# The first layer's modulation made feature tile by feature tile, with the first projection unit summed over open banks as its tiles come

## The chip, the cores and the metric

The kernel runs on one core of one Trainium2 chip (trn2). The metric is the device time of one execution in microseconds (us). The core's engines run side by side, each through its own list of instructions in a fixed order: TensorE (PE in the profile, PEld for its weight loads), VectorE (DVE), ScalarE (ACT), GpSimd (POOL) and SyncE (SP), which issues the transfers. An instruction that waits for another engine holds up all that stands behind it on its own engine.

## What is computed

The reference is one step of a two-layer trunk over 640 tokens of 1024 features: 512 sample tokens and 128 context tokens. In each layer the tokens are normalised, scaled and shifted by a modulation, and multiplied by a wide projection `w_in`; three mixers follow, then an output projection, a second modulated norm and a feed-forward part. The change touches only how the first of these steps begins, in layer 0:

```python
mod_ctx = (jax.nn.silu(c_ctx) @ w_mod[l] + b_mod[l])[None, None, :]
mod_lat = (jax.nn.silu(c) @ w_mod[l] + b_mod[l])[:, None, :]
sh1, sc1, g1, sh2, sc2, g2 = jnp.split(mod, 6, axis=-1)
h = rmsnorm(x, lp['norm1']) * (1 + sc1) + sh1
proj = h @ lp['w_in'] + lp['b_in']
```

`sh1` and `sc1` for all 1024 features need the first 2048 columns of `w_mod[0]`, which is 8 MB of the input. `h` can't be finished before them, and the projection multiplies `h`.

## The kernel before

Features lie on the 128 partitions, in KD = 8 feature tiles; tokens lie along the free dimension, in TT = 5 token tiles of 128 (four of the sample, one of the context). Every fp32 product of a large matrix is made of three products in fp32r: each operand is split into a rounded part and the rest (`split`, L215 to L218: ScalarE casts the rounded part, VectorE subtracts it, L217 and L218), and `gemm_a` and `gemm_b` (L183 to L213) issue three matmuls for each pair of tiles. In `gemm_b` these are L210 to L212, for one token tile t, with the token tile as the loaded weight and 272 (or 256, or 512) columns of the other operand moving.

`start` (L1604) is the opening stage of layer 0. It loads the transposed input `xT` in eight pieces, squares them (L1619) and adds the squares (L1621). Then `mod_first` (L278) loads `w_mod0`, the 2048 columns, in eight pieces `raw` of 1 MB through six buffers. Piece k holds 128 rows of the contraction and all 2048 columns, so each piece adds to all columns, and no column is finished before the eighth piece. Its products (L287) have two rows of output (sample and context) and stand in four groups of partitions, q = 0 to 3, of one PSUM bank. Behind the second piece the callback `after` loads the bias and norm columns (L1626) and puts `normalize` (L1632): sums over features by matmuls with ones (L1636), a power of -0.5 on GpSimd (L1639), a spread of the result over partitions by five diagonal matrices (L1643, L1644) into the tile `rb`, and eight multiplications of `xT[k]` by it (L1646). Behind the fifth it loads and splits the weights of the first projection unit (`first_w_in`, L1453: the columns ML_V with 16 gate columns, 272 in all).

When the eighth piece is in, the sums are copied (L291, L292), transposed (L295), and biased into columns (L299); `mod_norm_cols` (L335) makes the scale A. Then, in two banks of tokens (256 and 384), each feature tile is modulated (L1658 on ScalarE, L1660 on VectorE) and split into the act tiles.

`drive` (L514) runs the projection units one by one. The first is made by `unit_b` (L434): for each token tile t, `gemm_b` sums over the eight feature tiles into a bank of its own and `consume` (L604 and L610) adds the biases on the way out. A unit's weights are loaded (L141) and split while the one before it runs. The first unit's bias rows `vb` and `gb` are loaded by L589 and L591, and the mask tiles `mlm` by L1354; all three lie in a pool that reuses the memory of `start`'s pool. `ml_gates` (L653) starts with five transposes (L667) when the first unit's gate columns are done.

PSUM has eight banks: two tiles `mm`, two `t`, and two `s2` of two banks each. `mm_ps` (L106) gives an `mm` tile, and while `ff_phase` is true it gives `t` and `mm` by turns, by a flag `self.alt` that flips at every call; it is true in the first unit of a layer and in the feed-forward parts. There `ff1_evac` (L443) reads the sums (L1447), `ff2` (L1534), and a background task (`mod_chunk_dve`, L308) makes the later modulations with transposes into `t` tiles (L330).

The order of the instructions on each engine is fixed when the kernel is built: from those whose operands are expected to be ready, the one that stands first in the program goes first, so the order in time is not that of the program text.

Of the kernel before, what the change touches and what calls it, by code (L numbers as in the profile page):

```python
# [11 lines left out]
F32 = mybir.dt.float32  # L12
F32R = mybir.dt.float32r
AF = mybir.ActivationFunctionType
ALU = mybir.AluOpType
AX = mybir.AxisListType
# [3 lines left out]
P = 128  # L20
D = 1024
KD = D // P
DEPTH = 2
NS = 512
NT = 640
TT = 5
SPLIT = 256
BANKS = ((0, SPLIT), (SPLIT, NT))
# [3 lines left out]
EPS = 1e-6  # L32
BIG = 1.0e30
DA_Q, DA_K, DA_V = 0, 512, 1024
ML_Q, ML_K, ML_V, ML_O, ML_G = 1536, 2048, 2560, 3072, 3584
# [5 lines left out]
ROW_N1, ROW_N2, ROW_SUB, ROW_MLN, ROW_G, ROW_SN = 96, 104, 112, 113, 117, 118  # L41
# [45 lines left out]
class Builder:  # L87
# [187 lines left out]
        return (hb if half else cv)[:, i:i + 1]  # L275


    def mod_first(self, after):  # L278

        nc, I = self.nc, self.I  # L280
        ps = self.mm_ps()
        nc.vector.memset(ps, 0.0)
        for k in range(KD):
            raw = self.T(self.xp, [P, 2048], F32, "raw8", 6)
            nc.sync.dma_start(raw, I["w_mod0"][k])
            for q in range(4):
                nc.tensor.matmul(ps[32 * q:32 * q + 2, :], self.cc3[:, :, k], raw[:, q * 512:(q + 1) * 512],  # L287
                                 start=(k == 0), stop=(k == KD - 1))
            after(k)
        row = self.T(self.xp, [P, 512], F32, "modrow", 1)  # L290
        nc.vector.tensor_copy(row[:, :256], ps[:, :256])  # L291
        nc.scalar.copy(row[:, 256:], ps[:, 256:])  # L292
        tp = self.mm_ps()
        for j in range(4):
            nc.tensor.transpose(tp[:, j * P:(j + 1) * P], row[:, j * P:(j + 1) * P], self.ident)  # L295
        t4 = tp.rearrange("p (j q z) -> p j q z", j=4, q=4)
        jq = lambda x: x.rearrange("p (q j) -> p j q", q=4)
        for v in range(2):
            nc.vector.tensor_tensor(jq(self.modc[0][:, v, 0:16]), t4[:, :, :, v], jq(self.colv[0][1][:, 0:16]), op=ALU.add)  # L299

    def mod_store(self, l, n, src):
        nc = self.nc
        cv2 = self.colv[l][1]
# [130 lines left out]
    def unit_b(self, c0, consume, extra=None):  # L434

        def prep():
            return self.w_bmode(self.in_blk(self.l, c0), extra=extra)

        def run(w):
            for t in range(TT):  # L440
                consume(t, self.gemm_b(w, self.act, t))
                yield
        return prep, run, None  # L443

# [1158 lines left out]

    def start(self):  # L1604

        tc, nc, I = self.tc, self.nc, self.I
        with tc.tile_pool(name="xp_in", bufs=1, reuse_waits="tile") as xp:
            self.xp = xp
            loads, fin = self.load_cols(0)
            self.xsrc = [I["x_sample"][0, t * P:(t + 1) * P] for t in range(4)] + [I["x_prompt"][0]]  # L1610
            xT = [self.hd() for _ in range(KD)]
            ws = []
            ones = self.T(xp, [P, P], F32, "ones", 1)
            nc.gpsimd.memset(ones, 1.0)
            acc = self.T(xp, [P, NT], F32, "acc", 1)
            for k in range(KD):
                nc.sync.dma_start(xT[k], I["xT"][:, k])
                sq = acc if k == 0 else self.T(xp, [P, NT], F32, "sq", 2)
                nc.scalar.activation(sq, xT[k], AF.Square)  # L1619
                if k:  # L1620
                    nc.vector.tensor_tensor(acc, acc, sq, op=ALU.add)  # L1621

            def after(k):
                if k == 1:
                    for o, i in loads:
                        nc.sync.dma_start(o, i)  # L1626
                    fin()
                    normalize()
                if k == 4:
                    ws.append(self.first_w_in(0)())  # L1630

            def normalize():  # L1632

                ps = self.t_ps()
                for t in range(TT):
                    nc.tensor.matmul(ps[:, 2 * t:2 * t + 2], acc[:, t * P:(t + 1) * P], ones[:, :2], start=True, stop=True)  # L1636
                ss, r = self.st(5), self.st(5)
                nc.vector.tensor_scalar(ss, ps[:, 0:2 * TT:2], 1.0 / D, EPS, op0=ALU.mult, op1=ALU.add)
                nc.gpsimd.tensor_tensor(r, ss, self.mhalf[:, :TT], op=ALU.pow)  # L1639
                rb = self.s_ps()  # L1640
                for t in range(TT):
                    dg = self.T(xp, [P, P], F32, "diag", 2)
                    nc.vector.tensor_scalar_mul(dg, self.ident, r[:, t:t + 1])  # L1643
                    nc.tensor.matmul(rb[:, t * P:(t + 1) * P], ones, dg, start=True, stop=True)  # L1644
                for k in range(KD):
                    nc.vector.tensor_tensor(xT[k], xT[k], rb[:, :NT], op=ALU.mult)  # L1646
            self.mod_first(after)
            w, = ws
            A, B = self.mod_norm_cols(0, 0)
            act = [(self.act_slice(), self.act_slice()) for _ in range(KD)]  # L1650
            for a, b in BANKS:
                for k in range(KD):
                    x = xT[k]
                    for v, c0, c1 in ((0, a, min(b, NS)), (1, max(a, NS), b)):
                        if c0 >= c1:
                            continue
                        if a > 0 and v == 0 or a == 0 and k % 3 == 1:
                            nc.scalar.activation(x[:, c0:c1], x[:, c0:c1], AF.Identity, scale=A[:, v, k:k + 1], bias=B[:, v, k:k + 1])  # L1658
                        else:
                            nc.vector.tensor_scalar(x[:, c0:c1], x[:, c0:c1], A[:, v, k:k + 1], B[:, v, k:k + 1],  # L1660
                                                    op0=ALU.mult, op1=ALU.add)
                    hi, lo = act[k]
                    self.split(hi[:, a:b], lo[:, a:b], x[:, a:b])
        return act, w

    def run(self):
        tc, nc, I = self.tc, self.nc, self.I
# [48 lines left out]
def lay_out(x):  # L1716
# [4 lines left out]
    def blocks(w, n):  # L1721

        k, m = w.shape[1:]
        return w.reshape(L, k // P, P, m // n, n).transpose(0, 3, 2, 1, 4)

    def halves(w):
# [10 lines left out]
    a = {  # L1737
        "w_in": blocks(np.concatenate([w_in[:, :, :ML_G], w_in[:, :, NA_Q:]], axis=2), 256),
        "w_g": blocks(w_in[:, :, ML_G:NA_Q], 16)[:, 0],
        "w_ff1": blocks(x["w_ff1"], 256),  # L1740
        "w_up_da": blocks(x["w_up_da"], 256),
        "w_up_ml": blocks(x["w_up_ml"], 256),
        "w_up_na": blocks(x["w_up_na"], 256),
        "w_out": halves(x["w_out"]),
        "w_ff2": halves(x["w_ff2"]),
        "w_mod": x["w_mod"].reshape(L, 2, 4, P, 12, 512).transpose(0, 4, 1, 3, 2, 5),
        "w_mod0": x["w_mod"][0, :, :2048].reshape(KD, P, 2048),
        "xT": xs.T.reshape(KD, P, NT).transpose(1, 0, 2),
        "x_sample": x["x_sample"],
        "x_prompt": x["x_prompt"],  # L1750
# [36 lines left out]
```

## Time and profile before

| | us |
|---|---|
| median of 3 runs | 2488.46 |
| lowest and highest run | 2487.56, 2493.28 |
| the profiled execution, its own time | 2490.52 |
| span of that execution, first to last instruction | 2488.7 |
| TensorE busy in it | 2415.0 (97%) |

The profiled execution took 1.8 us outside its span, and 2.06 us more than the median. In the profile a group names line, engine and operation, and out<-in by the program's tile names: `mm`, `t` and `s` are PSUM, `act` is any 128 x 640 tile of the main pools (the input tiles `xT` among them), `raw` is a loaded weight, `whi` and `wlo` its two parts.

### The profile page before, as it was taken

The page shows a single profiled execution, that of the slowest core. Times are in us where ns is not written, and L with a number is a line of the kernel's source. Part 1 is how long each engine was busy: PE and PEld are TensorE (multiplying, and loading weights), DVE is VectorE, ACT ScalarE, POOL GpSimd, SP SyncE. Part 2 cuts the span into 40 slices and gives each one's busy share as a digit, 9 for nine tenths or more (in the row PEclk, how much of TensorE's full clock was granted, in tenths as well). Part 3 has the DMA queues.
Part 4 walks back from the last instruction along what each step waited for, and adds up shares of the span by engine and source line. Part 5 has one row for each costly group of instructions (what it writes and reads, how often), then busy time and mean ns, then how long its engine had stood idle before and what let it go on. Part 6 is the DMA issues. An engine that isn't in the chain of part 4 may idle for free. (4 is left out here: it accounts for less than half of the span.)

```text
span 2488.7 us, 39544 instructions
## 1 busy us (share of the span) xinstructions
PE 2415.0 (97%) x15776; PEld 2266.3 (91%) x15776; DVE 1523.0 (61%) x2804; ACT 905.1 (36%) x1954; POOL 640.9 (26%) x701
## 2 busy tenths in 40 slices
PE   6999999999999999999999999999999999999998
PEld 4999999999998898999989999999989889999997
DVE  5557788566634899998565547674443464444444
ACT  4332354334433422223353334443443353322232
POOL 0122122233412233332021212222352312233301
PEclk8999999999999999999999999999999999999999
DMA  7323323333353334444332222223232722222221
GB/s 271 105 94 117 112 97 135 121 117 123 139 190 130 119 136 152 153 136 153 103 122 97 96 90 87 76 82 111 74 116 86 261 85 85 68 85 68 85 68 60
DMA packets 73706, 286.52 MB, mean 115 GB/s; under 512 B 9889, under 2 KB 21249, under 8 KB 49969
## 3 DMA queue, kind: packets, MB, share of 16 engines
q1 hardware_dynamic: 73520, 283.99, 33.3%
q8 instruction: 124, 2.03, 0.3%
q14 instruction: 62, 0.50, 0.1%
HBM read 257.60 MB, written 26.35 MB: 114 GB/s over the span
## 5 line engine op out<-in xcount | busy, mean ns | idle before, releaser
L191 PE MATMUL mm<-act,whi 128*128 128x384 f32 (+1 forms) x2176 | 699.4, 321 | 11.7 <-DVE act L503 3.4
L192 PE MATMUL mm<-act,whi 128*128 128x384 f32 (+1 forms) x2176 | 687.5, 316 | 0.0
L193 PE MATMUL mm<-act,wlo 128*128 128x384 f32 (+1 forms) x2176 | 686.0, 315 | 0.0
L217 ACT CAST whi<-raw 128x1024 fp32r<-128x1024 f32 x296 | 310.9, 1050 | 921.3 <-PE mm L192 439.3
L218 DVE TENSOR_TENSOR wlo<-raw,whi 128x1024 fp32r<-128x1024 f32 x296 | 383.8, 1297 | 381.3 <-ACT whi L217 327.2
L191 PEld LDWEIGHTS mm<-act,whi 128*128 128x128 f32 x2176 | 413.9, 190 | 17.5 <-issue 6.0
L192 PEld LDWEIGHTS mm<-act,whi 128*128 128x128 f32 x2176 | 414.3, 190 | 0.0
L193 PEld LDWEIGHTS mm<-act,wlo 128*128 128x128 f32 x2176 | 413.8, 190 | 0.0
L1535 POOL TENSOR_TENSOR x<-x,tmp 128x512 f32<-128x512 f32 x120 | 194.0, 1623 | 448.5 <-DVE tmp L1534 448.5
L210 PE MATMUL mm<-whi,act 128*128 128x256 f32 (+2 forms) x800 | 270.0, 338 | 0.0
L212 PE MATMUL mm<-whi,act 128*128 128x256 f32 (+2 forms) x800 | 267.1, 334 | 0.0
L211 PE MATMUL mm<-wlo,act 128*128 128x256 f32 (+2 forms) x800 | 266.4, 333 | 0.0
L323 DVE SCALAR_TENSOR_TENSOR macc<-raw,cc,macc 128x512 f32<-128x512 f32 x280 | 232.2, 874 | 20.0 <-DMA raw<-w_mod 19.6
L212 PEld LDWEIGHTS mm<-whi,act 128*128 128x128 f32 x800 | 152.0, 190 | 14.3
L211 PEld LDWEIGHTS mm<-wlo,act 128*128 128x128 f32 x800 | 152.1, 190 | 14.0
L210 PEld LDWEIGHTS mm<-whi,act 128*128 128x128 f32 x800 | 152.1, 190 | 14.0
L210 PE MATMUL t<-whi,act 128*128 128x512 f32 (+1 forms) x416 | 158.5, 381 | 1.7 <-ACT act L217 1.5
L211 PE MATMUL t<-wlo,act 128*128 128x512 f32 (+1 forms) x416 | 157.8, 379 | 0.0
L212 PE MATMUL t<-whi,act 128*128 128x512 f32 (+1 forms) x416 | 157.8, 379 | 0.0
L192 PE MATMUL t<-act,whi 128*128 128x256 f32 (+1 forms) x512 | 146.4, 286 | 0.0
L193 PE MATMUL t<-act,wlo 128*128 128x256 f32 (+1 forms) x512 | 146.4, 286 | 0.0
L191 PE MATMUL t<-act,whi 128*128 128x256 f32 (+1 forms) x512 | 146.2, 286 | 0.0
(286 smaller groups left out, 4168.6 us busy)
## 6 DMA issues: line engine op xcount, KB each, us to landing
raw<-w_in SPq DMA_DIRECT2D x64, 1024.0 KB
raw<-w_ff SPq DMA_DIRECT2D x64, 1024.0 KB
raw<-w_mod SPq DMA_DIRECT2D x48, 1024.0 KB
mgd<-act SPq DMA_DIRECT2D x32, 320.0 KB
act<-mgd SPq DMA_DIRECT2D x32, 320.0 KB
raw<-w_out SPq DMA_DIRECT2D x8, 1024.0 KB
gr<-gd SPq DMA_DIRECT2D x12, 512.0 KB
act<-rd SPq DMA_DIRECT2D x16, 320.0 KB
```

The lines of the kernel that those rows point to most:

```text
L191: nc.tensor.matmul(o, wh, ah, start=(k == 0), stop=False)
L192: nc.tensor.matmul(o, wh, al, start=False, stop=False)
L193: nc.tensor.matmul(o, wl, ah, start=False, stop=(k == nk - 1))
L210: nc.tensor.matmul(o, ah, wh, start=(first and k == 0), stop=False)
L211: nc.tensor.matmul(o, ah, wlo, start=False, stop=False)
L212: nc.tensor.matmul(o, al, wh, start=False, stop=(last and k == nk - 1))
L217: self.nc.scalar.copy(hi, src)
L218: self.nc.vector.tensor_tensor(lo, src, hi.bitcast(F32), op=ALU.subtract)
L323: nc.vector.scalar_tensor_tensor(acc[v], r3[:, k, :], s, acc[v], op0=ALU.mult, op1=ALU.add)
L1535: nc.gpsimd.tensor_tensor(xs[t][:, sl], xs[t][:, sl], tmp, op=ALU.add)
```

## The change

`mod_first` goes. The 2048 columns of `w_mod0` are laid out anew: piece j now holds all 1024 rows of the contraction, and the 128 shift and 128 scale columns of feature tile j, so a piece gives a finished tile of modulation. The products of a piece are eight matmuls of 256 columns, two rounds over the four groups of partitions (`mod_products`); ScalarE copies the four partial rows out, and two matmuls with a selecting matrix `sel` add the four groups and turn them into columns (`mod_apply`), for which VectorE makes shift B and scale A of tile j. ScalarE modulates the context's 128 tokens, VectorE the sample's 512, and the tile is split. The first projection unit runs with the feature tile as its outer loop: `project(j)` adds tile j's 15 matmuls of 272 columns to five sums that stay open in five banks (two `mm`, two `t`, half an `s2`). The unit's weights are loaded behind the second piece, and `start` hands the sums on, so that the unit in `drive` only reads them out. The bias columns are loaded ahead of the first piece.

```diff
--- before.py
+++ after.py
@@ -275,29 +275,6 @@
         return (hb if half else cv)[:, i:i + 1]
 
 
-    def mod_first(self, after):
-
-        nc, I = self.nc, self.I
-        ps = self.mm_ps()
-        nc.vector.memset(ps, 0.0)
-        for k in range(KD):
-            raw = self.T(self.xp, [P, 2048], F32, "raw8", 6)
-            nc.sync.dma_start(raw, I["w_mod0"][k])
-            for q in range(4):
-                nc.tensor.matmul(ps[32 * q:32 * q + 2, :], self.cc3[:, :, k], raw[:, q * 512:(q + 1) * 512],
-                                 start=(k == 0), stop=(k == KD - 1))
-            after(k)
-        row = self.T(self.xp, [P, 512], F32, "modrow", 1)
-        nc.vector.tensor_copy(row[:, :256], ps[:, :256])
-        nc.scalar.copy(row[:, 256:], ps[:, 256:])
-        tp = self.mm_ps()
-        for j in range(4):
-            nc.tensor.transpose(tp[:, j * P:(j + 1) * P], row[:, j * P:(j + 1) * P], self.ident)
-        t4 = tp.rearrange("p (j q z) -> p j q z", j=4, q=4)
-        jq = lambda x: x.rearrange("p (q j) -> p j q", q=4)
-        for v in range(2):
-            nc.vector.tensor_tensor(jq(self.modc[0][:, v, 0:16]), t4[:, :, :, v], jq(self.colv[0][1][:, 0:16]), op=ALU.add)
-
     def mod_store(self, l, n, src):
         nc = self.nc
         cv2 = self.colv[l][1]
@@ -437,8 +414,9 @@
             return self.w_bmode(self.in_blk(self.l, c0), extra=extra)
 
         def run(w):
+            sums, w = w if isinstance(w, tuple) else (None, w)
             for t in range(TT):
-                consume(t, self.gemm_b(w, self.act, t))
+                consume(t, self.gemm_b(w, self.act, t) if sums is None else sums[t])
                 yield
         return prep, run, None
 
@@ -1603,15 +1581,17 @@
 
     def start(self):
 
+
         tc, nc, I = self.tc, self.nc, self.I
         with tc.tile_pool(name="xp_in", bufs=1, reuse_waits="tile") as xp:
             self.xp = xp
             loads, fin = self.load_cols(0)
             self.xsrc = [I["x_sample"][0, t * P:(t + 1) * P] for t in range(4)] + [I["x_prompt"][0]]
             xT = [self.hd() for _ in range(KD)]
-            ws = []
             ones = self.T(xp, [P, P], F32, "ones", 1)
             nc.gpsimd.memset(ones, 1.0)
+            sel = self.T(xp, [P, 2], F32, "sel", 1)
+            nc.vector.tensor_reduce(sel, self.ident.rearrange("p (q z) -> p z q", q=4)[:, 0:2], axis=AX.X, op=ALU.add)
             acc = self.T(xp, [P, NT], F32, "acc", 1)
             for k in range(KD):
                 nc.sync.dma_start(xT[k], I["xT"][:, k])
@@ -1619,49 +1599,85 @@
                 nc.scalar.activation(sq, xT[k], AF.Square)
                 if k:
                     nc.vector.tensor_tensor(acc, acc, sq, op=ALU.add)
-
-            def after(k):
-                if k == 1:
-                    for o, i in loads:
-                        nc.sync.dma_start(o, i)
-                    fin()
-                    normalize()
-                if k == 4:
-                    ws.append(self.first_w_in(0)())
-
-            def normalize():
-
-                ps = self.t_ps()
+            for o, i in loads:
+                nc.sync.dma_start(o, i)
+            raws, w = [], None
+            for j in range(KD):
+                raw = self.T(xp, [P, 2048], F32, "raw8", 6)
+                raws.append((raw, raw.rearrange("p (k c) -> p k c", k=KD)))
+                nc.sync.dma_start(raws[j][1], I["w_mod0"][j])
+                if j == 1:
+                    wraw = self.w_raw(self.in_blk(0, ML_V))
+                    rx = self.T(self.wp, [P, 8, 16], F32, "rx", 1)
+                    nc.sync.dma_start(rx, I["w_g"][0])
+
+
+            ps = self.t_ps()
+            for t in range(TT):
+                nc.tensor.matmul(ps[:, 2 * t:2 * t + 2], acc[:, t * P:(t + 1) * P], ones[:, :2], start=True, stop=True)
+            ss, r = self.st(5), self.st(5)
+            nc.vector.tensor_scalar(ss, ps[:, 0:2 * TT:2], 1.0 / D, EPS, op0=ALU.mult, op1=ALU.add)
+            nc.gpsimd.tensor_tensor(r, ss, self.mhalf[:, :TT], op=ALU.pow)
+            rb = self.s_ps()
+            for t in range(TT):
+                dg = self.T(xp, [P, P], F32, "diag", 2)
+                nc.vector.tensor_scalar_mul(dg, self.ident, r[:, t:t + 1])
+                nc.tensor.matmul(rb[:, t * P:(t + 1) * P], ones, dg, start=True, stop=True)
+            fin()
+            cv, cv2, _ = self.colv[0]
+            sc1 = self.T(self.cst, [P, KD], F32, "sc1", 1)
+            nc.gpsimd.tensor_scalar(sc1, cv2[:, 8:16], 1.0, None, op0=ALU.add)
+            mps = self.s_ps()
+            nc.vector.memset(mps, 0.0)
+            A = self.T(self.cst, [P, 2, KD], F32, "modA", 2)
+            B = self.modc[0][:, :, 0:8]
+            act = [(self.act_slice(), self.act_slice()) for _ in range(KD)]
+            rows = [None] * KD
+
+            def mod_products(j):
+
+                o = mps[:, (j % 2) * 256:(j % 2) * 256 + 256]
+                for k in range(KD):
+                    q = k % 4
+                    nc.tensor.matmul(o[32 * q:32 * q + 2], self.cc3[:, :, k], raws[j][1][:, k], start=(k < 4), stop=(k >= 4))
+                rows[j] = self.T(xp, [P, 256], F32, "modrow", 2)
+                nc.scalar.copy(rows[j], o)
+
+            def mod_apply(j):
+
+                c = mps[:, 512 + 4 * j:516 + 4 * j]
+                for g in range(2):
+                    nc.tensor.matmul(c[:, 2 * g:2 * g + 2], rows[j][:, g * P:(g + 1) * P], sel, start=True, stop=True)
+                nc.vector.tensor_scalar(B[:, :, j], c[:, 0:2], cv2[:, j:j + 1], None, op0=ALU.add)
+                nc.vector.tensor_scalar(A[:, :, j], c[:, 2:4], sc1[:, j:j + 1], cv[:, ROW_N1 + j:ROW_N1 + j + 1],
+                                        op0=ALU.add, op1=ALU.mult)
+                x = xT[j]
+                hi, lo = act[j]
+                nc.scalar.activation(x[:, NS:], x[:, NS:], AF.Identity, scale=A[:, 1, j:j + 1], bias=B[:, 1, j:j + 1])
+                for a, b in BANKS if j == KD - 1 else ((0, NT),):
+                    e = min(b, NS)
+                    nc.vector.tensor_scalar(x[:, a:e], x[:, a:e], A[:, 0, j:j + 1], B[:, 0, j:j + 1], op0=ALU.mult, op1=ALU.add)
+                    self.split(hi[:, a:b], lo[:, a:b], x[:, a:b])
+
+            sums = [self.mm_ps(), self.mm_ps(), self.t_ps(), self.t_ps(), self.s_ps()[:, :512]]
+            sums = [o[:, :272] for o in sums]
+
+            def project(j):
                 for t in range(TT):
-                    nc.tensor.matmul(ps[:, 2 * t:2 * t + 2], acc[:, t * P:(t + 1) * P], ones[:, :2], start=True, stop=True)
-                ss, r = self.st(5), self.st(5)
-                nc.vector.tensor_scalar(ss, ps[:, 0:2 * TT:2], 1.0 / D, EPS, op0=ALU.mult, op1=ALU.add)
-                nc.gpsimd.tensor_tensor(r, ss, self.mhalf[:, :TT], op=ALU.pow)
-                rb = self.s_ps()
-                for t in range(TT):
-                    dg = self.T(xp, [P, P], F32, "diag", 2)
-                    nc.vector.tensor_scalar_mul(dg, self.ident, r[:, t:t + 1])
-                    nc.tensor.matmul(rb[:, t * P:(t + 1) * P], ones, dg, start=True, stop=True)
-                for k in range(KD):
-                    nc.vector.tensor_tensor(xT[k], xT[k], rb[:, :NT], op=ALU.mult)
-            self.mod_first(after)
-            w, = ws
-            A, B = self.mod_norm_cols(0, 0)
-            act = [(self.act_slice(), self.act_slice()) for _ in range(KD)]
-            for a, b in BANKS:
-                for k in range(KD):
-                    x = xT[k]
-                    for v, c0, c1 in ((0, a, min(b, NS)), (1, max(a, NS), b)):
-                        if c0 >= c1:
-                            continue
-                        if a > 0 and v == 0 or a == 0 and k % 3 == 1:
-                            nc.scalar.activation(x[:, c0:c1], x[:, c0:c1], AF.Identity, scale=A[:, v, k:k + 1], bias=B[:, v, k:k + 1])
-                        else:
-                            nc.vector.tensor_scalar(x[:, c0:c1], x[:, c0:c1], A[:, v, k:k + 1], B[:, v, k:k + 1],
-                                                    op0=ALU.mult, op1=ALU.add)
-                    hi, lo = act[k]
-                    self.split(hi[:, a:b], lo[:, a:b], x[:, a:b])
-        return act, w
+                    self.gemm_b([w[j]], [act[j]], t, sums[t], first=(j == 0), last=(j == KD - 1))
+            for j in range(KD):
+                if j == 0:
+                    for k in range(KD):
+                        nc.vector.tensor_tensor(xT[k], xT[k], rb[:, :NT], op=ALU.mult)
+                mod_products(j)
+                if j == 1:
+                    w = self.w_bmode_split(wraw, rx)
+                if j >= 2:
+                    project(j - 2)
+                mod_apply(j)
+            project(KD - 2)
+            project(KD - 1)
+        return act, (sums, w)
 
     def run(self):
         tc, nc, I = self.tc, self.nc, self.I
@@ -1744,7 +1760,7 @@
         "w_out": halves(x["w_out"]),
         "w_ff2": halves(x["w_ff2"]),
         "w_mod": x["w_mod"].reshape(L, 2, 4, P, 12, 512).transpose(0, 4, 1, 3, 2, 5),
-        "w_mod0": x["w_mod"][0, :, :2048].reshape(KD, P, 2048),
+        "w_mod0": x["w_mod"][0, :, :2048].reshape(KD, P, 2, KD, P).transpose(3, 1, 0, 2, 4).reshape(KD, P, KD, 2 * P),
         "xT": xs.T.reshape(KD, P, NT).transpose(1, 0, 2),
         "x_sample": x["x_sample"],
         "x_prompt": x["x_prompt"],
```

## Rows read from the trace of the kernel before

**Rows 1.** The page, busy time and share of the span by engine.

```profile
PE 2415.0 (97%) x15776; PEld 2266.3 (91%) x15776; DVE 1523.0 (61%) x2804; ACT 905.1 (36%) x1954; POOL 640.9 (26%) x701
```

**Rows 2.** Windows: us, busy (instructions) by engine, granted PE clock, DMA share, GB/s.

```profile
25.00:30.00 5.00, 2.19 (x24) 0.30 (x16) 5.00 (x9) 2.28 (x4) 0.00 (x0) 1.00 1.02 415
30.00:35.00 5.00, 2.95 (x20) 0.22 (x16) 1.41 (x4) 0.00 (x0) 0.10 (x1) 0.54 1.01 419
35.00:40.00 5.00, 2.86 (x13) 1.03 (x6) 2.19 (x9) 1.69 (x5) 1.61 (x9) 0.50 0.51 161
```

**Rows 3.** Timeline of PE, 13 to 37 us: start, length, instruction, count [idle before, releaser].

```profile
13.59 2.27 PE L1636 MATMUL t<-ones,acc 128*128 128x2 f32 x10 [13.59 <-DVE acc L1621]
...
18.94 1.89 PE L287 MATMUL mm<-raw,cc 128*2 128x512 f32 x8
...
22.66 4.05 PE L287 MATMUL mm<-raw,cc 128*2 128x512 f32 x32
29.52 1.06 PE L287 MATMUL mm<-raw,cc 128*2 128x512 f32 x8 [2.81 <-DMA raw<-w_mod]
32.02 1.88 PE L287 MATMUL mm<-raw,cc 128*2 128x512 f32 x8 [1.44 <-DMA raw<-w_mod]
34.52 1.89 PE L287 MATMUL mm<-raw,cc 128*2 128x512 f32 x8 [0.61 <-DMA raw<-w_mod]
```

**Rows 4.** Windows of the first projection unit.

```profile
39.63:44.00 4.37, 4.37 (x19) 4.37 (x20) 4.37 (x15) 4.37 (x12) 0.00 (x0) 0.50 0.84 265
44.00:56.77 12.77, 12.77 (x103) 12.77 (x102) 9.32 (x25) 8.90 (x17) 0.00 (x0) 1.00 0.26 83
```

**Rows 5.** Timeline of PE, in the first unit and right behind it.

```profile
40.93 0.43 PE L212 MATMUL mm<-whi,act 128*128 128x272 f32 x1
...
41.15 0.43 PE L210 MATMUL t<-whi,act 128*128 128x272 f32 x1
...
56.77 0.60 PE L667 MATMUL s<-ident,act 128*100 128x128 f32 x4
```

**Rows 6.** Timeline of DVE, 22 to 30 us.

```profile
22.77 1.55 DVE L1646 TENSOR_TENSOR act<-act,s 128x640 f32<-128x640 f32 x2 [0.89 <-PE s L1644]
...
24.34 4.47 DVE L1646 TENSOR_TENSOR act<-act,s 128x640 f32<-128x640 f32 x6
...
28.79 1.22 DVE L218 TENSOR_TENSOR wlo<-raw,whi 128x1024 fp32r<-128x1024 f32 x1
29.92 0.22 DVE L218 TENSOR_TENSOR wlo<-rx,whi 128x64 fp32r<-128x64 f32 x1
```

**Rows 7.** Groups of 0 to 60 us, by form: count | busy us, mean ns | idle before.

```profile
L1619 ACT ACTIVATE sq<-act 128x640 f32<-128x640 f32 x7 | 5.2, 736 | 2.0 <-DMA act<-xT 1.6 <-DVE acc L1621 0.2
L1660 DVE TENSOR_SCALAR act<-act,modA,modc 128x128 f32<-128x128 f32 x8 | 2.5, 342 | 0.0
L1660 DVE TENSOR_SCALAR act<-act,modA,modc 128x256 f32<-128x256 f32 x5 | 1.8, 410 | 0.0
L343 DVE SCALAR_TENSOR_TENSOR modA<-modc,colv 128x16 f32<-128x16 f32 x1 | 0.2, 174 | 0.0
```

**Rows 8.** Timeline of SP's issues.

```profile
16.50 8.04 SPq L285 DMA_DIRECT2D raw<-w_mod  x3
24.58 0.42 SPq L141 DMA_DIRECT2D raw<-w_in  x1
...
36.46 0.83 SPq L1354 DMA_DIRECT2D mlm<-k_mlm  x2
37.34 0.43 SPq L589 DMA_DIRECT2D vb<-b_in  x1
```

**Rows 9.** Source views of L1447, L1534 and L330: count, ns min/median/max, first to last, forms.

```profile
L1447 ACT ACTIVATE relu<-t,colv x64: 453/473/579, 818.7 to 2422.3; 128x256 f32<-128x256 f32 x60, 128x384 f32<-128x384 f32 x4
...
L1534 DVE TENSOR_TENSOR tmp<-t,gr x60: 673/684/692, 851.1 to 2367.5; 128x512 f32<-128x512 f32 x60
...
L330 PE MATMUL t<-ident,macc x160: 270/273/329, 232.2 to 1196.0; 128*128 128x128 f32 x160
```

## The prediction

> **What bounds the kernel now.** I read the page first. TensorE is busy for 97% of the span [rows 1], so time is saved where it stands idle, or where it works at a low clock. The windows over the first 60 us come next, since the change lies there. From 25 to 35 us the transfers take the whole of the DMA engines (share 1.01 and 1.02), while TensorE is busy for 2.19 and 2.95 us of 5, and its clock falls to 0.50 [rows 2], the lower of its two levels, 1.2 GHz. The timeline shows why: its products of the modulation wait for their pieces, which land every 2.5 us, the last at 34.5 [rows 3]. These end at 36.41 (34.52 + 1.89), and the first projection unit starts at 39.63. From there TensorE has no gap: 4.37 us at clock 0.50, then 12.77 at 1.00 [rows 4], until the gate transposes at 56.77 [rows 5]. So 17.14 us hold the unit's 120 matmuls: 4.37/19 = 0.23 us each at the low clock, 12.77/103 = 0.124 at the high one. The unit's end at 56.77 is what the change can move. Everything behind it runs on a TensorE that is nearly always busy, so I pass on a shift of this point to the end unchanged.
>
> **The change part by part.** *The wait removed.* Projection need no longer stand behind the eighth piece. The question is when tile 0 is ready, and here VectorE decides, not the transfers. The normalisation's spread ends at 22.7, and eight multiplications of `xT` run from 22.77 to 28.81 [rows 6]. The change writes all eight ahead of tile 0's modulation, and all become ready at one moment, so I expect them in the same place and at the same price. Then for tile 0: scale and shift, two small operations at 0.17 each (as L343); the modulation of 512 tokens, which the trace has only at 128 and 256 columns (342 and 410 ns), so 410 + 2 x 68 = 0.55; on ScalarE a cast of 640 columns, 0.74 (the square of that shape) [rows 7]; and the rest by subtraction, 0.75 (4.47/6, the nearest row of that shape [rows 6]). The cast ends at 28.81 + 0.34 + 0.55 + 0.74 = 30.4, the subtraction at 31.2 or, behind the first half of the weights' split (1.22 and 0.22 [rows 6]), at 31.9. The first of the three matmuls needs only the cast. I take 31.0 for the start of projection: 8.6 us earlier than now. If both halves of the weights' split go first (28.79 to 31.4 now), it is 33.
>
> *The work added inside the unit's time.* The products cost in total what they did: 16 passes of 256 columns in place of 8 of 512, both four groups of partitions side by side. Eight passes take 4.05/4 = 1.01 us in the group of 32, and 1.88 or 1.89 at the low clock [rows 3]. But now some of them stand between the projection's matmuls. The chain that holds them back is in the code: a product shares its bank with the copy of the piece before; the two row buffers let copy j + 2 start only after selection j; and selection j shares its bank with the reading of scale and shift j - 1. Scale and shift 1 stand behind the weights' split, which ends at about 33. So pieces 5, 6 and 7 can't be done ahead, and selections 2 to 7 neither. Three products cost 3 x 1.01 = 3.0. A selection is two matmuls in two passes each, with 128 x 128 fp32 weights and two columns; the nearest row is the sums with ones, ten such passes in 2.27 us, 0.91 for four [rows 3]. The first products, at 18.94, also took the 1.89 of the low clock, although the windows give 1.00 for those early slices; so I take 0.91 for the low clock and half of it, rounded to 0.5, for the high one. Six selections: 3.0.
>
> *The sum.* 31.0 + 17.1 (the same 120 matmuls, the same slow beginning) + 3.0 + 3.0 = 54.1, against 56.77: 2.7 us less. The profiled execution took 2490.5 (span 2488.7 and 1.8 around it); it would be 2487.8. From the median of the runs, 2488.5, I get 2485.8. Bounds: with a start at 33, four products at 1.89 and seven selections at 0.91 the unit ends at 33 + 17.1 + 7.6 + 6.4 = 64.1, 7.3 us later (2495.8). With a start at 30.4 and nothing between, it ends at 47.5, 9.3 us earlier (2479.2).
>
> *The clock.* Before, the clock was 0.50 while TensorE was half idle and rose during 4.37 us of unbroken projection [rows 2, 4]. In the sum TensorE is unbroken from 31 on, so it should rise again, and I count the slow beginning once. The Trainium skill speaks against the change here: "TensorE: Matmul & The Clock Gate", section "Loop structure matters more than you think", calls a loop that waits for a transfer ahead of each matmul the bad one, because the clock drops, and wants all contraction tiles back to back. By the row the sum stays at 2485.8; by the rule, taken to the letter, the whole unit would be slow, which is a rival below.
>
> *Edits costed at nothing.* The transfers: the same bytes, and the weights of the unit were already ahead of the last pieces. The sixth to eighth pieces are issued from 16.50 to 24.54, as buffers come free [rows 8]; the last lands at 34.5 and is not wanted until about 48 in my sum, so even a piece or two of delay is covered. ScalarE's share for a tile (copy, context, cast) and VectorE's (0.34 + 0.55 + 0.75 = 1.6 us) fit beside TensorE's 1.9 + 1.0 + 0.5. SyncE is the place where something is late next: it now stops at the masks (L1354) until `start`'s memory is free, at 36.46 just behind the last product [rows 8]. In my sum this comes at about 49 or 50, and behind it stand `vb`, 0.9 later, and `gb`, which the first read-out needs at 52.6. At the 161 GB/s of the window around their present issue [rows 2], 256 KB are 1.6 us: about on time. I take nothing, and at most 3 us if the read-out, and the second unit's bank with it, is late.
>
> *A side effect.* `mm_ps` was called seven times up to the end of the unit and is now called twice. The flag is left the other way round, and through the feed-forward parts `mm` and `t` change places: the sums of 256 columns, 60 of 64 in `t` now, would be in `mm`. The background's 160 transposes also want `t` [rows 9]. I take nothing, since both have two banks; the bound is a wait for one read-out (0.68 [rows 9]) at each of the 24 pairs of them that I place in the first feed-forward part, 16 us, and a gain as unlikely.
>
> **The rivals.** *First, tile 0 overtakes seven of the multiplications* (faster). Then it is cast at 22.77 + 0.78 + 0.34 + 0.55 + 0.74 = 25.2, with its weights near 25.8, while the clock is still 1.00 [rows 2]. The unit is 120 x 0.124 = 14.9; with four products and seven selections, 25.8 + 14.9 + 4.0 + 3.5 = 48.2, 8.5 us less: 2480.0. For it: it takes only another order on VectorE. Against: program order.
>
> *Second, products broken up* (slower). The trace has matmuls of two token tiles one by one in turn [rows 5]. If products and projection are mixed like that, the groups of partitions no longer overlap: eight passes of four groups in 1.01 us make about 0.5 for one alone at 512 columns, 0.25 at 256, and 16 x 0.25 = 4.0 for a piece instead of 1.0. It turns slower by more than 7.5 us from four such pieces on: 2485.8 + 4 x 3.0 = 2497.8. Against: the eight products of a piece become ready together.
>
> *Third, the stop-and-go clock* (slower). If every tile waits and the clock never rises, 120 x 0.23 + 3 x 1.89 + 6 x 0.91 = 38.7 from 31.0 on, an end at 69.7 and 2501.4. It decides if TensorE is idle between tiles; my sums give 3.4 us of its work for each 1.6 of VectorE's.
>
> *Fourth, the change gives nothing*: projection starts at 33 behind both weight halves, four products and seven selections fall into it: 33 + 17.1 + 4.0 + 3.5 = 57.6, or 2489.3.
>
> *Fifth, the exchanged banks* cost in the feed-forward part: at 16 us 2501.8, at half of it still within 0.3%.
>
> **How the numbers follow.** About 0.3% (7.5 us: below 2481.0 or above 2495.9) is what a measurement of this kernel can tell from no change. My forecast has 0.58, with its own range 2481 to 2491; the first rival 0.15, the second 0.06, the third 0.03, the fourth 0.14, the fifth 0.04. Of the forecast, 0.02 spill over to faster and 0.01 to slower. So faster 0.17, same 0.69, slower 0.14. The range goes from the first rival, 2479, to the dear end of the sum, 2496.
>
> **What would show it.** Right: the multiplications end near 28.8; the first L210 at about 31; products of pieces 5 to 7 and their selections between projection's matmuls; clock 1.00 from about 35; the gate transposes near 54; the 256-column sums of the feed-forward part in `mm`. Wrong: a first L210 before 27, or L667 after 57; single products between projection's matmuls; a read-out that waits for `vb`; TensorE waits at L330 that were not there.

## The result, and the profile after

The change makes the kernel slower: 2513.64 us in the median (2506.85 to 2515.62) against 2490.28, a ratio of 1.0089 with the interval [1.0064, 1.0113]. I had forecast 2485.8, which is 2.7 us faster, in a range from 2479 to 2496, and given slower 0.14. It came out 23.4 us slower. The profiled execution has a span of 2513.4 us; the last output is issued at 2509.8 instead of 2485.2, so 24.6 us are to be found.

TensorE's share is what it was [rows 1], its time 13.4 us more:

```profile
PE 2428.4 (97%) x15868; PEld 2278.8 (91%) x15868; DVE 1529.8 (61%) x2806; ACT 906.2 (36%) x1951; POOL 641.1 (26%) x702
```

Such a page can't say where. Landmarks can: one and the same instruction in both traces. The first gate transpose comes at 59.0 instead of 56.8, the first feed-forward sum of layer 0 is read at 820.8 instead of 818.7, the last of the background's transposes stands at 1221.1 instead of 1196.0, and the last output comes 24.6 later. So in this pair of executions the opening that was rewritten ends about 2 us later, the same 2 us are there behind the mixers, and some 23 us arise in layer 0's feed-forward part, of which no line was changed.

Two windows of that part, which hold 2174 matmuls each, first of the kernel before and then of the changed one (us, then busy and count for PE, PEld, DVE, ACT and POOL, granted clock, DMA share, GB/s):

```profile
819.00:1197.00 378.00, 375.40 (x2174) 343.58 (x2174) 339.96 (x489) 114.38 (x196) 122.53 (x68) 1.00 0.42 142
```
```profile
821.00:1222.00 401.00, 385.61 (x2174) 352.09 (x2173) 343.26 (x489) 115.08 (x196) 121.92 (x68) 0.97 0.39 133
```

TensorE's idle time went from 2.6 us (378.00 - 375.40) to 15.4, and the matmuls took 10.2 us longer, with a mean clock of 0.97 instead of 1.00. Together 23.0. TensorE's waits in that part, in the changed kernel (us in total, times, longest):

```profile
PE t L307 <- DVE tmp L1512: 8.0, 6, 2.9
PE t L191 <- DVE st L308: 5.7, 6, 1.1
PE s L367 <- POOL xn L361: 1.8, 2, 1.2
```

and in the kernel before:

```profile
PE s L390 <- POOL xn L384: 1.8, 2, 1.2
PE t L330 <- DVE tmp L1534: 0.8, 1, 0.8
```

L307, L308 and L1512 are the old L330, L331 and L1534: the background's transposes, their reduction by VectorE, and `ff2`'s read-out. All new waits, 12.9 us (8.0 + 5.7 - 0.8), are for `t` banks: transposes that wait until VectorE has read out a sum of `ff2`, and behind them sums of the feed-forward part (L191) that wait until VectorE has reduced the transposes (L308). The source view shows that `mm` and `t` have changed places, against [rows 9]:

```profile
L1425 ACT ACTIVATE relu<-mm,colv x64: 458/473/578, 820.8 to 2446.9; 128x256 f32<-128x256 f32 x60, 128x384 f32<-128x384 f32 x4
```

How one such wait comes about is seen in the timelines around one pair of transposes. VectorE before:

```profile
933.25 1.78 DVE L323 SCALAR_TENSOR_TENSOR macc<-raw,cc,macc 128x512 f32<-128x512 f32 x1
934.95 0.68 DVE L1534 TENSOR_TENSOR tmp<-t,gr 128x512 f32<-128x512 f32 x1
935.55 1.21 DVE L218 TENSOR_TENSOR wlo<-raw,whi 128x1024 fp32r<-128x1024 f32 x1
936.68 0.68 DVE L1534 TENSOR_TENSOR tmp<-mm,gr 128x512 f32<-128x512 f32 x1
```

VectorE after, and then TensorE after:

```profile
937.66 2.43 DVE L300 SCALAR_TENSOR_TENSOR macc<-raw,cc,macc 128x512 f32<-128x512 f32 x2
940.02 0.68 DVE L1512 TENSOR_TENSOR tmp<-mm,gr 128x512 f32<-128x512 f32 x1
940.62 1.21 DVE L218 TENSOR_TENSOR wlo<-raw,whi 128x1024 fp32r<-128x1024 f32 x1
941.75 0.68 DVE L1512 TENSOR_TENSOR tmp<-t,gr 128x512 f32<-128x512 f32 x1
```
```profile
938.95 0.60 PE L307 MATMUL t<-ident,macc 128*128 128x128 f32 x4
942.49 1.11 PE L307 MATMUL t<-ident,macc 128*128 128x128 f32 x4 [2.94 <-DVE tmp L1512]
943.25 0.56 PE L191 MATMUL mm<-act,whi 128*128 128x256 f32 x1
```

The background needs two `t` banks one after the other, for each of the twelve chunks of modulation that it makes in this part; every second chunk waits, once in each round of some 62 us. Two sums of `ff2` are still to be read out by VectorE, with a weight subtraction of 1.21 us between them. Before, the sum in `t` was read first; now it is the later of the two, and the second four transposes wait for it, with all of TensorE's work behind them. The clock follows (windows of the changed kernel):

```profile
942.50:945.00 2.50, 2.26 (x9) 1.97 (x10) 2.50 (x3) 0.00 (x0) 2.50 (x2) 0.50 0.69 292
945.00:947.50 2.50, 2.50 (x9) 2.50 (x9) 2.50 (x7) 0.00 (x0) 0.16 (x1) 0.50 0.96 318
947.50:950.00 2.50, 2.50 (x12) 2.50 (x11) 2.50 (x5) 0.00 (x0) 0.00 (x0) 0.67 0.27 108
950.00:955.00 5.00, 5.00 (x37) 5.00 (x36) 3.39 (x6) 2.94 (x5) 0.00 (x0) 1.00 0.54 184
```

After 2.94 us of idling TensorE works at the low level, 1.2 GHz, for some 6 us more. That is 3 us of work lost, so by this estimate a wait of 3 us costs about twice itself. The Trainium skill, "TensorE: Matmul & The Clock Gate", section "Why this matters for your kernels", asks to avoid long idle gaps between bursts of matmuls, because the clock falls behind one; this trace agrees, with the granted clock of 0.50 behind the 2.94 us above, but here shorter gaps lowered it too (last section).

The opening itself, one line of VectorE's timeline after (L1671 are the eight multiplications by the norm), then TensorE's (L1642 are the products, L1650 the selections, L645 the gate transposes):

```profile
21.28 5.94 DVE L1671 TENSOR_TENSOR act<-act,s 128x640 f32<-128x640 f32 x8 [0.89 <-PE s L1625]
```
```profile
23.55 1.01 PE L1650 MATMUL s<-sel,modrow 128*128 128x2 f32 x4 [0.49 <-ACT modrow L1644]
27.59 1.89 PE L1642 MATMUL s<-raw,cc 128*2 128x256 f32 x16 [3.03 <-DVE modA L1652]
29.99 0.59 PE L210 MATMUL mm<-whi,act 128*128 128x272 f32 x1 [0.52 <-ACT act L217]
...
33.86 1.27 PE L1642 MATMUL s<-raw,cc 128*2 128x256 f32 x16
...
37.28 1.04 PE L1642 MATMUL s<-raw,cc 128*2 128x256 f32 x16
...
50.91 1.05 PE L1642 MATMUL s<-raw,cc 128*2 128x256 f32 x16
...
58.09 0.29 PE L212 MATMUL s<-whi,act 128*128 128x272 f32 x1
59.05 0.29 PE L645 MATMUL s<-ident,act 128*100 128x128 f32 x1 [0.66 <-DVE act L582]
```

Projection starts at 29.99 and ends at 58.4 (58.09 + 0.29). In between stand six pieces of products, from 33.86 to 50.91 one every 3.4 us, for 15 projection matmuls, a selection and the products themselves. Seven selections stand there too.

### The profile page after: what moved, and what is told of

It reads as the page before. It is cut to its first block, busy times and chain, and to the rows that moved or that the text cites. A ratio compares the mean times of both kernels' runs of the same rounds, so it can differ in the third digit from the quotient of the medians.

```text
span 2513.4 us, 39746 instructions
## 1 busy us (share of the span) xinstructions
PE 2428.4 (97%) x15868; PEld 2278.8 (91%) x15868; DVE 1529.8 (61%) x2806; ACT 906.2 (36%) x1951; POOL 641.1 (26%) x702
## 4 chain that ended last, share of the span: by engine, by line
PE 73%; DVE 9%; issue 4%; DMA 3%; POOL 3%; ACT 1%; SPq 0%; POOLq 0%; DVEq 0%
PE mm L191 11%; PE mm L192 11%; PE mm L193 11%; PE mm L211 4%; PE mm L212 4%; PE mm L210 4%; PE t L191 4%; PE t L192 3%; PE t L193 3%; DVE macc L300 3%; PE t L212 2%; PE t L211 2%; PE t L210 2%; DVE wlo L218 2%; DMA raw<-w_mod 2%
## 5 line engine op out<-in xcount | busy, mean ns | idle before, releaser
L191 PE MATMUL mm<-act,whi 128*128 128x256 f32 (+1 forms) x2176 | 675.7, 311 | 13.7 <-DVE act L1149 5.2
L192 PE MATMUL mm<-act,whi 128*128 128x256 f32 (+1 forms) x2176 | 663.2, 305 | 0.0
L193 PE MATMUL mm<-act,wlo 128*128 128x256 f32 (+1 forms) x2176 | 662.7, 305 | 0.0
L191 PEld LDWEIGHTS mm<-act,whi 128*128 128x128 f32 x2176 | 415.0, 191 | 20.2 <-issue 7.3
L210 PE MATMUL mm<-whi,act 128*128 128x256 f32 (+2 forms) x808 | 273.2, 338 | 1.0 <-ACT act L217 0.9
L212 PE MATMUL mm<-whi,act 128*128 128x256 f32 (+2 forms) x808 | 269.4, 334 | 0.0
L191 PE MATMUL t<-act,whi 128*128 128x384 f32 (+1 forms) x512 | 174.2, 340 | 5.7 <-DVE st L308 5.7
L192 PE MATMUL t<-act,whi 128*128 128x384 f32 (+1 forms) x512 | 173.0, 338 | 0.0
L193 PE MATMUL t<-act,wlo 128*128 128x384 f32 (+1 forms) x512 | 172.7, 337 | 0.0
L210 PE MATMUL t<-whi,act 128*128 128x512 f32 (+1 forms) x400 | 153.4, 384 | 0.0
L212 PE MATMUL t<-whi,act 128*128 128x512 f32 (+1 forms) x400 | 152.9, 383 | 0.0
```

Of the source, the lines that this page charges most:

```text
L191: nc.tensor.matmul(o, wh, ah, start=(k == 0), stop=False)
L192: nc.tensor.matmul(o, wh, al, start=False, stop=False)
L193: nc.tensor.matmul(o, wl, ah, start=False, stop=(k == nk - 1))
L210: nc.tensor.matmul(o, ah, wh, start=(first and k == 0), stop=False)
L212: nc.tensor.matmul(o, al, wh, start=False, stop=(last and k == nk - 1))
```

## The experiments

The kernel before was measured again beside these runs: its median was 2490.47 us beside the first four and 2489.37 beside the last three (the flag in layer 1 and the two runs on the norm). The ratios are against these.

**The flag alone, in the kernel before.** The first question is whether the exchange of the banks makes the loss without anything of the new opening.

```diff
             self.ff_phase = True
+            if l == 0:
+                self.alt = not self.alt
             AB = self.mod_norm_cols(l, 1)
```

> The kernel before, with one edit: the flag that gives mm and t banks by turns is turned over once at the start of layer 0's feed-forward part. Nothing of the opening is touched. Theory (the exchange of mm and t banks is the loss): from the changed kernel's landmarks 22.7 of its 25 us lie between the first feed-forward sums and the last background transposes, so this kernel takes about 2490 + 22.7 = 2513 us, TensorE waits at the transposes (L330) for the read-outs of ff2 (L1534) and at t sums for L331, some 13 us in all, and the clock of that stage drops from 1.00 to about 0.97. Rival (the opening's shift of 2 us puts VectorE and the loads of the feed-forward part out of step, and the banks do no harm): 2490 us, no such waits.

Measured: 2511.58 us, ratio 1.0081 [1.0066, 1.0096]. The waits of that part (L330 and L331 as before, L1536 is the old L1534):

```profile
PE t L330 <- DVE tmp L1536: 8.2, 6, 2.7
PE t L191 <- DVE st L331: 6.1, 6, 1.1
PE s L390 <- POOL xn L384: 1.8, 2, 1.2
```

The theory holds: two lines that compute nothing bring back nearly the whole loss, with the same waits. A window of the part gives 16.1 us of idle time in 401 (384.91 busy) and a clock of 0.98.

**The flag turned back, in the changed kernel.** The same two lines.

> The changed kernel with the same one-line turn of the flag, so that mm and t stand in the feed-forward part as in the kernel before. Theory (bank exchange): the 22.7 us go and the opening's 2.1 to 2.3 us stay: 2490.3 + 2.3 = 2492.6 us, waits at L307 as few as before (0.8 us). Rival (opening out of step): 2513 us as the changed kernel.

Measured: 2489.84 us, 0.9998 [0.9989, 1.0007]; one wait at L307, 0.9 us. The loss is gone. The 2.3 us that the opening was to leave (0.0009 of 2490) don't show: the interval ends at 1.7 us slower. Its profiled execution does come later, with the gate transposes at 60.2 and the last output at 2488.4 against 2485.2, but that execution is the slowest of its ten.

**Products free of scale and shift.** On top of the turned flag:

```diff
-                rows[j] = self.T(xp, [P, 256], F32, "modrow", 2)
+                rows[j] = self.T(xp, [P, 256], F32, "modrow", 8)
...
-                c = mps[:, 512 + 4 * j:516 + 4 * j]
+                c = last[:, 512 + 4 * j:516 + 4 * j]
...
-            sums = [self.mm_ps(), self.mm_ps(), self.t_ps(), self.t_ps(), self.s_ps()[:, :512]]
+            last = self.s_ps()
+            sums = [self.mm_ps(), self.mm_ps(), self.t_ps(), self.t_ps(), last[:, :512]]
```

> As the run before it (flag turned), and two things more in the opening: the columns that the selection writes lie in the free bank beside the fifth sum, not beside the products, and eight row buffers stand in place of two, so that no product waits for scale and shift of the tile before. Theory (products 1 to 7 were held behind scale and shift, one at 27.59 after a wait of 3.0 us for L1652, so that seven of them at 1.05 us fell into the unit's time): pieces 1 and 2 are now done ahead, the first projection starts near 30 as before, and the gate transposes come 2 us earlier, near 57 instead of 59.0: 2490.5 us. Rival (VectorE alone sets when tiles are ready, TensorE has room for the products): gate transposes still at 59, 2492.6 us.

Measured: 2490.85 us, 0.9999 [0.9989, 1.0008]. In its trace the second piece's products follow the first's, and the gate transposes come at 57.46, 1.6 us earlier than in the changed kernel, whose opening gives 59.0, 60.2 and 60.9 in the three executions that have it unchanged:

```profile
21.02 1.84 PE L1644 MATMUL s<-raw,cc 128*2 128x256 f32 x16
23.35 1.05 PE L1644 MATMUL s<-raw,cc 128*2 128x256 f32 x16 [0.50 <-ACT modrow L1646]
...
57.46 0.29 PE L645 MATMUL s<-ident,act 128*100 128x128 f32 x1 [0.67 <-DVE act L582]
```

So the wait of 3.03 us for L1652 was what held the second piece back. Only pieces 1 and 2 moved ahead, as expected, which leaves five in the unit's time. The third piece now stands from 29.70 on ahead of the first projection matmul, which comes at 31.52 and not near 30 as I expected. The later ones keep their places between projections in the order fixed at build, though the DMA engines are done at about 35 us. The kernel's time doesn't resolve a gain of this size.

**The background's transposes in another bank.** The changed kernel, flag untouched.

```diff
-            tp = self.t_ps()
+            tp = self.s_ps()[:, :512] if self.ff_phase else self.t_ps()
```

> The changed kernel with the flag as the change leaves it, but the background's transposes of the feed-forward part go to an s2 tile in place of a t tile. Theory (they collide with feed-forward sums in t): the collision is gone whichever way the flag stands, about 2492 us, no waits at L307 for L1512. Rival A (the exchanged banks hurt by themselves, through the order of the read-outs): 2513 us. Rival B (the s2 tile is wanted by the second norm at the start of the part): a few us above 2492 with the waits at L367 grown from 5.3 us.

Measured: 2488.72 us, 0.9992 [0.9983, 1.0002]. The feed-forward part has only the 1.8 us of waits at the second norm, which were there before, and clock 1.00. Banks in exchanged places do no harm if the transposes don't want one of them. But this edit also gains something of its own. From the first feed-forward sum to the last of the background's transposes its execution takes 374.3 us (823.2 to 1197.5), and those of the two runs on the norm, which keep the edit, 374.5 and 374.4; the kernel before, the changed kernel with the flag turned back, the run with free products and that with the flag in layer 1 take 377.2 to 377.5. Of the 3 us, 0.8 is the wait at the transposes; what the rest is isn't shown. So the time of this run doesn't say that the new opening costs nothing.

**The flag turned in layer 1 instead.** In the kernel before, with `if l == 1`. There the feed-forward sums are exchanged too, but the background has run out of work: its last transposes stand at 1197.6.

> The kernel before with the flag turned over at the start of layer 1's feed-forward part instead of layer 0's. There mm and t change places just the same, but no background work runs beside it any more. Theory (only the background's transposes collide with the exchanged sums): no effect, 2490 us. Rival (exchanged banks delay the feed-forward read-outs as such): layer 1's part loses some 10 to 23 us as layer 0's did, 2500 to 2513 us.

Measured: 2489.42 us, 0.9999 [0.9990, 1.0008]. The exchange is there, half of the 256-column sums being in `mm` now:

```profile
L1447 ACT ACTIVATE relu<-mm,colv x64: 472/527/586, 824.8 to 2424.3; 128x256 f32<-128x256 f32 x32, 128x384 f32<-128x384 f32 x32
```

TensorE's waits in layer 1's part are those of the kernel before, 2.5 and 1.8 us. No effect, so it takes the background's transposes and the exchange together.

**Tile 0 early.** The changed kernel with the transposes in `s2`, the edits of the products, and the norm made tile by tile:

```diff
+            rbs = self.T(xp, [P, NT], F32, "rbs", 1)
+            nc.scalar.copy(rbs, rb[:, :NT])
...
-                if j == 0:
-                    for k in range(KD):
-                        nc.vector.tensor_tensor(xT[k], xT[k], rb[:, :NT], op=ALU.mult)
+                nc.vector.tensor_tensor(xT[j], xT[j], rbs, op=ALU.mult)
```

> The changed kernel with the background's transposes in an s2 tile, the selection's columns beside the fifth sum, eight row buffers, and the first rival of the prediction made true: the spread norm is copied out of PSUM by ScalarE, and each feature tile is multiplied by it just ahead of its own modulation, not all eight ahead of tile 0. Theory (VectorE's eight multiplications of 5.9 us hold tile 0 back, TensorE is the bound from there): projection starts near 26 instead of 30, the unit then needs 15 for its matmuls, about 6 x 1.05 for products, 7 x 0.5 for selections and 2 for the low clock at its start, so the gate transposes come near 53 to 54 instead of 59 to 61, and the kernel takes 2488.7 - 6 = about 2483 us. Rival (the loads are the bound once tile 0 is early, since TensorE's products stand in its order between the projections): gate transposes at 56 or later, 2486 us or more.

Measured: 2490.91 us, 1.0004 [0.9995, 1.0013]. My expectation of 2483 fell. TensorE's timeline and then its windows:

```profile
27.57 0.82 PE L210 MATMUL mm<-whi,act 128*128 128x272 f32 x2 [1.52 <-ACT whi L217]
28.19 0.65 PE L210 MATMUL t<-whi,act 128*128 128x272 f32 x2
29.99 0.59 PE L211 MATMUL mm<-wlo,act 128*128 128x272 f32 x1 [0.92 <-DVE wlo L218]
31.88 1.73 PE L1642 MATMUL s<-raw,cc 128*2 128x256 f32 x16
...
58.50 0.29 PE L645 MATMUL s<-ident,act 128*100 128x128 f32 x1 [1.80 <-DVE act L582]
```
```profile
25.00:30.00 5.00, 2.12 (x10) 1.71 (x10) 5.00 (x11) 4.40 (x8) 0.00 (x0) 0.65 1.01 421
30.00:35.00 5.00, 5.00 (x34) 3.47 (x35) 2.92 (x6) 0.38 (x1) 0.00 (x0) 0.67 1.02 420
35.00:40.00 5.00, 5.00 (x48) 4.11 (x46) 3.87 (x8) 2.43 (x5) 0.00 (x0) 1.00 0.15 49
```

The first matmul comes at 27.57, but now the unit's weights are late: TensorE waits for ScalarE's cast and then for VectorE's subtraction of them. Behind that it works through a stretch at clock 0.67 and has all six later pieces in its way. The gate transposes come at 58.50, where the rival had them. Half of the rival's reason holds, the products that stand between the projections; the other half doesn't: the loads are over at 35 (DMA share 0.15), while TensorE stays full. At the end it idles 1.80 us, because on VectorE the second unit's weight subtractions (55.90 to 58.18) stand ahead of the read-outs.

**The shift merged into the split**, on top of that:

```diff
-                nc.scalar.activation(x[:, NS:], x[:, NS:], AF.Identity, scale=A[:, 1, j:j + 1], bias=B[:, 1, j:j + 1])
...
+                for v, a, e in ((0, 0, NS), (1, NS, NT)):
+                    nc.vector.scalar_tensor_tensor(x[:, a:e], x[:, a:e], A[:, v, j:j + 1], rbs[:, a:e], op0=ALU.mult, op1=ALU.mult)
+                    nc.scalar.activation(hi[:, a:e], x[:, a:e], AF.Identity, bias=B[:, v, j:j + 1])
+                    nc.vector.scalar_tensor_tensor(lo[:, a:e], x[:, a:e], B[:, v, j:j + 1], hi[:, a:e].bitcast(F32), op0=ALU.add, op1=ALU.subtract)
```

> As the run with the norm made tile by tile, with the shift moved out of VectorE's and ScalarE's modulation: VectorE multiplies by scale and norm in one instruction, ScalarE adds the shift while it makes the rounded part, VectorE adds it while it subtracts. If VectorE still sets the pace of the tiles, this comes 1 to 2 us ahead of the run before it; if TensorE does, the two are alike within 1 us, near 2483 us.

Measured: 2490.45 us, 1.0005 [0.9996, 1.0014]: like the run before it within 1 us, but neither is near 2483. That TensorE sets the pace isn't shown by this: in the profiled execution the whole opening is later, with the gate transposes at 62.6 instead of 58.5, and yet the first feed-forward sum comes at 821.9 against 821.5. No version here beats the kernel before by more than the measurement can tell.

## Why the prediction was wrong

*The step that failed* is the side effect, "I take nothing, since both have two banks". I had seen that the flag would be left the other way round and that the transposes want `t`, made it the fifth rival with a bound of 16 us, and gave it 0.04. It was this rival, and at 23 us. Two of my signs of being wrong came with it, waits at the background's transposes and gate transposes after 57. That the exchange makes the loss without anything of the new opening is shown by the flag turned in the kernel before (2511.58 us), and that it takes the transposes in `t` by the run with them in `s2` (2488.72). Two thoughts were missing. First, the exchange isn't neutral on the average: the background takes the same number of steps in each round of the feed-forward part, so its transposes meet the same sums in every round (six rounds, six waits at L307, six at L191). Whether they meet a bank that VectorE has read out already could have been looked up before, in the timeline at 935: the read-out of `t` ahead of the weight subtraction, that of `mm` behind it. Second, the bound of 16 us counted 24 waits of 0.68 at the transposes alone. There were six, 8.0 us in all and up to 2.94, because other VectorE work stands between two read-outs, and six more of 5.7 us at the sums behind them. Together, 13.7 us, they stayed within the bound, by luck; what went beyond it is the fall of the clock, 10.2 us on top of 12.8 of new idle time, to which I had given no price.

*The opening.* Tile 0 was rightly placed, in part by luck: VectorE's multiplications ended at 27.2 and not at 28.8, but the first half of the weights' subtraction (27.45, 1.22 us) went ahead of the modulation, and the first projection matmul came at 29.99 (I said 31.0). The unit's end was not: 58.4 instead of 54.1, and so it lasted 28.4 us instead of 23.1. The mis-sized term is the work that falls into its time. I had counted three pieces of products, there are six, 1.04 to 1.27 us each, 3.5 us more than my 3.0; I had counted six selections, there are seven, 0.50 each as I took them but 0.85 for the first inside, 0.9 us more. These are 4.4 of the 5.3 us; 0.34 is a wait for tile 7's cast at 55.98, and the rest I can't place. The chain of shared banks and row buffers was stronger than I had it, since the second piece already waited for scale and shift 0 (3.03 us). But it accounts for one piece alone: with the chain cut, five still fell into the unit's time, where the order fixed at build puts them. My dear bound, 64.1, held the end.

*The clock in the opening.* My third rival didn't come. From 30 to 55 us TensorE is busy in the whole of every window in the changed kernel, and the matmuls are 0.23 us apart at first and 0.12 from about 35 on. There was no wait for a transfer between the tiles, so this run doesn't test what the Trainium skill says of loops that have one ("TensorE: Matmul & The Clock Gate", section "Loop structure matters more than you think").

*The edits costed at nothing* cost nothing: `vb` is issued at 52.95 and `gb` at 53.36, and the first read-out (58.73) follows a weight subtraction without a wait. The pass-on of a shift held in this pair of executions, 2.2 us at the gate transposes and 2.1 at 820, but so close by chance: the old opening's three executions take 761.9, 763.0 and 764.7 us from the one to the other.

What stays open is the opening's net worth. In profiled executions it ends 2 to 5 us later than before (gate transposes at 59.0, 60.2 and 60.9 with the new opening, 55.6, 56.8 and 57.1 with the old), and the first feed-forward sum comes 0.5 to 4.5 us later (820.8, 823.1 and 823.2 against 818.7, 820.1 and 820.3). None of them shows the gain that I had forecast. The times of the kernels don't resolve it: the cleanest, with the flag turned back, goes from 2.7 us faster to 1.7 slower.

## What to carry to other kernels

Where tiles are handed out by turns, count the calls that a change removes or adds: an odd number exchanges banks in code that nobody touched, and the stage to look at is the one where something else wants one of them. A wait on TensorE should be priced with the low clock that can follow it: here 12.8 us of new idle time cost another 10.2. And work moved into the waiting time of a stage must come out of the busy part of it: here the projection started 9.6 us earlier (29.99 against 39.63), but took the products and selections into its own time.

## What was not expected of the hardware

Shorter gaps also lowered the clock, but not always. After 2.26 us of idling ahead of 1005.68 and 1.08 ahead of 1007.89 the granted clock was 0.65 in the window from 1006 to 1010 and 0.60 in that from 1010 to 1015. The other four rounds have nearly the same two waits each, 0.6 to 0.8 us at L307 and 1.1 at L191. Their windows in the changed kernel:

```profile
853.00:915.00 62.00, 60.11 (x340) 54.18 (x339) 51.28 (x69) 15.90 (x24) 22.12 (x13) 1.00 0.44 151
1043.00:1103.00 60.00, 58.25 (x331) 52.62 (x331) 54.18 (x74) 15.79 (x24) 20.67 (x12) 1.00 0.41 141
1103.00:1164.00 61.00, 59.32 (x330) 53.78 (x329) 53.25 (x73) 16.01 (x24) 20.18 (x11) 0.97 0.41 139
1164.00:1222.00 58.00, 56.23 (x330) 52.14 (x329) 50.93 (x73) 16.77 (x26) 15.32 (x9) 0.97 0.39 131
```

In two of them the clock stayed at 1.00, in two it fell for a while. So the length of the gaps alone doesn't decide it; what does isn't shown here.
